# A hybrid attention and convolution layer on one core: f32 weights split at each use, a scaling moved to ScalarE, a sum moved to the DMA, loads and products moved ahead

## The chip, the cores and the metric

The kernel runs on one core of one Trainium2 chip. The metric is the device time of one execution in microseconds (us). A core has TensorE (PE in the profile; PEld is its weight load), VectorE (DVE), ScalarE (ACT), GpSimd (POOL) and SyncE (SP), which work side by side, each through its own instructions in order. DMAs are issued from the queues of SP, ACT and POOL and move data between the chip's memory (HBM) and the on-chip buffer (SBUF); matmuls write to PSUM, which has 8 banks here.

## The reference

One inference step of one layer, for 2048 prompt tokens and 32 sample tokens of 1024 values:

```
h   = rmsnorm(x);  z = h @ w_in        # q | k | v | gate_a | B | C | u | gate_c | merge_a | merge_c
q, k = rope(rmsnorm(q)), rope(rmsnorm(k))
attn = softmax with sinks, 8 q heads and 2 kv heads of 64, each chunk of 64 tokens over itself and 2 chunks before
conv = causal convolution of C * u over 3 tokens
y_a = (attn * silu(gate_a)) @ w_attn_out
y_c = (B * conv * silu(gate_c)) @ w_conv_out
r   = x + (sigmoid(merge_a) * y_a + sigmoid(merge_c) * y_c) @ w_o
out = r + sigmoid(r @ w_ple_gate) * (p @ w_ple_proj)
```

The outputs are `out`, and the newest keys, values and convolution rows.

## The kernel before

All values are f32, and everything is kept transposed: 128 features by tokens. For precision each operand of a matmul is split in two halves of the type float32r, a rounded high part and the rest (`split`, L92 to L94: ScalarE casts the high part, VectorE subtracts to get the low one; `split_half`, L96 to L98, does the same with a factor of 0.5). Each product takes three matmuls: high by high, high by low, low by high.

**The start** (L559 to L605). Rows of p are multiplied by W_pp (`p_product`, L535: 6 matmuls into a bank, ScalarE copies the bank out, a DMA on ACT's queue stores it to `z_pp`). In the program, four of the eight products of tokens 0 to 511 come before the RMS norm of the first x and four after the first step of h @ W_in.

**Phase I** (to about 885 us) computes z = h @ W_in in two halves of tokens, with 7 products in place of 8 for each 2 x 2 of blocks (`run`, L479, L364 for the matmuls). The steps (`steps`, L108 to L120) go over 21 groups of weight columns in each half. Results go to scratch tensors in HBM: `z_q`, `z_ga`, `z_y` (the convolution branch, already gated), `z_t` (tanh of the merge gates).

**Phase II** (from about 885 us) first multiplies the convolution rows by W_B for blocks 0 and 1 (`yB`, L935 to L945), then p @ W_pp for blocks 2 and 3 (L946 to L955), then yB for blocks 2 and 3. The convolution rows are loaded and split by `conv_rows` (L926): for blocks 0 and 1 at L933, at the head of Phase II; for 2 and 3 after their p products (L954). Then it goes over the four blocks of 512 tokens (the last has 32 more). In each block: finish the block's attention; yA = attention @ W_A (L968 to L978), times the gate `ta` (loaded from `z_t`), plus the convolution's share by an accumulating DMA on POOL's queue (L974); split into m; r = x + m @ W_o (L982 to L992), stored to `z_r` and split; tanh(r @ W_pg / 2) (L995 to L1011). The last step reads `pp` (p @ W_pp) and `rs` (r) back from HBM, and VectorE makes (tanh + 1) * pp (L1005) and 0.5 * that + rs (L1007); a DMA stores the row.

**Attention** is a set of generators, one for each 128 tokens (`attention`, L715, `sink_attention`, L651). It is advanced between the products by `tick` (L875), from a list of due times written by hand (`plan`, L895 to L903). A tile is transposed by PE, normed, rotated on POOL (L742 to L774), transposed again; then per chunk of 64: the scores S (L659), the maximum (L663), the exponential with its row sums on ScalarE (L675), the reciprocal of the sums (L679), P scaled by it on VectorE (L684), the transposes of P (L693), P times V (L709), the gate (L811).

**Weights.** The order of all weights is a list (`worder`, L123 to L131). A weight of 128 x 512 f32 (256 KB) is loaded on SP's queue into a buffer `wr` (`load_w`, L163), two ahead, and split into a buffer `w` (512 KB, a ring of 7, `WB`), up to 7 ahead of its use (`prefetch`, L191). The weights of Phase II (keys "q") are used up to four times: W_A, W_o and W_pg once for each block, W_B once for each pair of blocks. At its first use such a weight is split, and the split pair is stored to HBM by a DMA on POOL's queue:

```
k = wkept[key[2:]] = dram.tile([P, 2, 4, P], F32R, tag=f"wk{i}", name=f"wk{i}")
nc.gpsimd.dma_start(out=k, in_=w)                 # L207
```

At each later use the pair is loaded back on POOL's queue (L202) and nothing is split.

**Buffers and order.** Rows of a block live in a ring of 13 buffers (`tmp`), longer-lived ones in a pool of 36 (`row`, `pair`). An instruction that needs a buffer waits until the last reader of the buffer's former content is done, and all that stands behind it on its queue waits too. The order of each engine's instructions is not quite that of the program: it is fixed when the kernel is built, by a list scheduler with a model of times (L1088).

Of the kernel before, what the change touches and what calls it, by code (L numbers as in the profile page):

```python
# [8 lines left out]
F32R = mybir.dt.float32r  # L9
AF = mybir.ActivationFunctionType  # L10
# [3 lines left out]
P = 128  # L14
# [24 lines left out]
def tile_hybrid_stream_step(ctx: ExitStack, tc: tile.TileContext, x, xT, pT, wu, consts, rope, ckT, cv_dup,  # L39
# [52 lines left out]
    def split(hi, lo, src):  # L92
        nc.scalar.copy(out=hi, in_=src)  # L93
        nc.vector.tensor_tensor(out=lo, in0=src, in1=hi.bitcast(F32), op=sub)  # L94
# [36 lines left out]
        worder += [("q", b, UPG + n, s) for n in range(8) for s in range(2)]  # L131
    wsum = {g: dram.tile([P, 4, 4, P], F32, tag=f"ws{g}", name=f"ws{g}") for g in range(G)}
    WS = {7: 0, 5: 1, 6: 2, 3: 3}

    wkept = {}
    raw_of, made, used = {}, [], [0]
    raws = [0]
    ahead = [4]
# [24 lines left out]
    def load_w(i):  # L163
        key = worder[i]
        if key[0] == "q":
            return load_quad(key[2], key[3], f"wr{i}")
        if key[0] == "pp":
            return load_quad(UPP + key[2] // 2, key[2] % 2, f"wr{i}")
        _, h, g, p = key
        _, _, u1, u2 = groups[g]  # L170
        if p in (1, 2):
            return load_quad(u1, p - 1, f"wr{i}")
        if h == 0:
            if g not in sums:
# [8 lines left out]
    firsts = {}  # L183
    for i, key in enumerate(worder):
        if key[0] == "q":
            firsts.setdefault(key[2:], i)

    def kept(i):
        return worder[i][0] == "q" and firsts[worder[i][2:]] < i

    def prefetch(upto):  # L191
        upto = min(upto, len(worder))
        while len(made) < upto:
            i = len(made)
            while raws[0] < min(i + 2, len(worder)):
                if not kept(raws[0]):
                    raw_of[raws[0]] = load_w(raws[0])
                raws[0] += 1
            w = wp.tile([P, 2, 4, P], F32R, tag="w", name=f"w{i}")
            key = worder[i]  # L200
            if kept(i):
                nc.gpsimd.dma_start(out=w, in_=wkept[key[2:]])  # L202
            else:
                split(w[:, 0], w[:, 1], raw_of.pop(i))
                if key[0] == "q":
# [329 lines left out]
    def p_product(name, n, t0, q, pa, wpp):  # L535
        t = tmp(f"pp{name}_{n}")
        for c0, cn in [(0, q)] if q <= 512 else [(0, q // 2), (q // 2, q // 2)]:
            ps = bank(f"pp{name}_{n}_{c0}")
            for k in range(2):
                for e, (a, c) in enumerate(((0, 0), (0, 1), (1, 0))):  # L540
                    nc.tensor.matmul(out=ps[:, :cn], lhsT=wpp(n, a, k), rhs=pa[k][c][:, c0:c0 + cn],  # L541
                                     start=k == 0 and e == 0, stop=k == 1 and e == 2)
# [10 lines left out]
    def finish(r):  # L553
        try:
            next(r)
        except StopIteration as e:
            return e.value

    X1 = second_half()  # L559
    pa = p_rows("0", 0, 512)  # L560
# [47 lines left out]
    for i, todo in enumerate(steps):  # L608
        if i < 8:
            continue  # L610
        if todo[0][:2] == (0, 0) and todo[0][2] in (7, 5, 3, 4):
            make_x(todo[0][2])
        run(todo)
        if i in prep:
            next(X1, None)
        for p in range(1, 8):
            if last[p] == i:
                if p == 1:
                    for _ in X1:
                        pass  # L620
                refill(p)
# [20 lines left out]
    def blk(b):  # L642
        t0, npr, ns = BLOCKS[b]
        nt = npr + ns
        subs = [(0, nt)] if nt <= 512 else [(0, nt // 2), (nt // 2, nt // 2)]
        tiles = [(ns + i * P, P) for i in range(npr // P)] + ([(0, ns)] if ns else [])
        return t0, npr, ns, nt, subs, tiles

    def sink_attention(name, ng, lhs, krhs, cn, e_out, norm, keys, sk, nsk, done):  # L651
# [28 lines left out]
        for kv in range(2):  # L680
            for j in range(ng):
                g = kv * ng + j
                for src, dst in norm(kv, j):
                    nc.vector.tensor_scalar(out=dst, in0=src, scalar1=se[:, g:g + 1], scalar2=None, op0=mul)  # L684
        yield
        w = ng * P
        pts = []
# [226 lines left out]
                nc.tensor.matmul(out=ps[:, :cn], lhsT=lo, rhs=a[0][:, c0:c0 + cn], start=False, stop=(i == n - 1))  # L914
        return [(ps, c0, cn) for ps, (c0, cn) in zip(pss, subs)]

    def load_row(name, src, b):
        t0, nt = BLOCKS[b][0], blk(b)[3]
        t = tmp(name)
        nc.sync.dma_start(out=t[:, :nt], in_=src[:, t0:t0 + nt])  # L920
        return t


    yc = {}

    def conv_rows(b):  # L926
        nt = blk(b)[3]
        for c in range(4):
            t = load_row(f"yc{b}_{c}", z_y[c], b)
            yc[b, c] = pair(f"ycs{b}_{c}")  # L930
            split_half(yc[b, c][0][:, :nt], yc[b, c][1][:, :nt], t[:, :nt])
# [25 lines left out]
    for b in range(len(BLOCKS)):  # L957
        t0, npr, ns, nt, subs, tiles = blk(b)
        last = b == len(BLOCKS) - 1
        finish_attention(b)  # L960
        ac = []
        for j in range(4):
            a = pair(f"ac{b}_{j}")
            split_half(a[0][:, :nt], a[1][:, :nt], ats[b][j][:, :nt])
            ac.append(a)

        mT = []
        for n in range(8):  # L968
            ta = load_row(f"ta{b}_{n}", z_t[0][n], b)
            w = next_w(("q", b, UY + n, 0))  # L970
            for ps, c0, cn in product(f"yA{b}_{n}", [w], ac, subs):
                nc.vector.scalar_tensor_tensor(out=ta[:, c0:c0 + cn], in0=ta[:, c0:c0 + cn], scalar=1.0,  # L972
                                               in1=ps[:, :cn], op0=add, op1=mul)
            nc.gpsimd.dma_start(out=ta[:, :nt], in_=z_t[1][n][:, t0:t0 + nt], accum_op=add)  # L974
            m = pair(f"m{b}_{n}")
            split_half(m[0][:, :nt], m[1][:, :nt], ta[:, :nt])
            mT.append(m)
            tick(2.8)  # L978


        rT = []
        for n in range(8):  # L982
            xr = tmp(f"xr{b}_{n}")
            nc.sync.dma_start(out=xr[:, :nt], in_=xT[n * P:(n + 1) * P, t0:t0 + nt])
            w = [next_w(("q", b, UO + n, s)) for s in range(2)]
            for ps, c0, cn in product(f"o{b}_{n}", w, mT, subs):
                nc.vector.tensor_tensor(out=xr[:, c0:c0 + cn], in0=ps[:, :cn], in1=xr[:, c0:c0 + cn], op=add)
            r = pair(f"r{b}_{n}")
            split(r[0][:, :nt], r[1][:, :nt], xr[:, :nt])
            nc.gpsimd.dma_start(out=z_r[n][:, t0:t0 + nt], in_=xr[:, :nt])  # L990
            rT.append(r)
            tick(5.6)  # L992


        for n in range(8):  # L995
            tg = tmp(f"tg{b}_{n}")
            pp = load_row(f"zp{b}_{n}", z_pp[n], b)
            rs = load_row(f"rsum{b}_{n}", z_r[n], b)
            w = [next_w(("q", b, UPG + n, i)) for i in range(2)]
            cut = last and n == 7  # L1000
            for ps, c0, cn in product(f"pg{b}_{n}", w, rT, subs):
                nc.scalar.activation(out=tg[:, c0:c0 + cn], in_=ps[:, :cn], func=AF.Tanh, scale=0.5)
                for o0, on in ([(c0, cn)] if cut else [(0, nt)] if c0 + cn == nt else []):
                    o = slice(o0, o0 + on)
                    nc.vector.scalar_tensor_tensor(out=tg[:, o], in0=tg[:, o], scalar=1.0, in1=pp[:, o],  # L1005
                                                   op0=add, op1=mul)
                    nc.vector.scalar_tensor_tensor(out=rs[:, o], in0=tg[:, o], scalar=0.5, in1=rs[:, o],  # L1007
                                                   op0=mul, op1=add)
# [89 lines left out]
```

## Time and profile before

| what | us |
|---|---|
| median of 3 runs | 1615.51 |
| lowest, highest | 1613.94, 1619.77 |
| the profiled execution | 1621.73 |
| its span, first to last instruction | 1620.0 |
| PE, DVE, ACT and POOL busy in it | 1563.2, 981.6, 628.8, 446.9 |

The profile shows one execution. Its page gives the busy time of each engine; further views give the same for chosen stretches with the clock that TensorE was granted and the load of the DMA engines, the groups of instructions (line, engine, operation, output <- inputs, shapes, count, busy us, mean ns, then the idle time before them and what ended it), who waited for whom, and the chain of work that ended last. Matmuls overlap, so that the mean of one is longer than the distance between two. L numbers are lines of the kernel before.

### The profile page before, as it was taken

What the parts mean: (1) busy time and instruction counts of PE and PEld (TensorE: products, weight loads), DVE (VectorE), ACT (ScalarE), POOL (GpSimd) and SP (SyncE); (2) the same over time, 40 slices, a digit from 0 to 9 for tenths busy, and PEclk for the clock granted to TensorE, in tenths of its full rate; (3) what the DMA queues carried; (4) which work ended last, traced back from release to release, by engine and by line L of the source; (5) the groups of instructions that cost most, each with busy time, mean ns of one, the idle gap of its engine ahead of it and who ended that gap; (6) DMA issues with size and microseconds to landing.
All of it is one profiled execution on the core that took longest, in us unless ns stands there. A gap on an engine that the chain in (4) does not pass through costs nothing.

```text
span 1620.0 us, 26331 instructions
## 1 busy us (share of the span) xinstructions
PE 1563.2 (96%) x9387; PEld 1391.0 (86%) x9387; DVE 981.6 (61%) x1932; ACT 628.8 (39%) x1470; POOL 446.9 (28%) x676
## 2 busy tenths in 40 slices
PE   6899999999999999999999999988998999999998
PEld 5688888888899999999999788966886888788998
DVE  7875667756763455554333676777877777764322
ACT  6544334543563333333444364344433334432111
POOL 3122112212100000010000561544455455642320
PEclk8999999999999999999999999998999999999999
DMA  7655446689885433334446977898988789979986
GB/s 260 227 197 187 153 153 198 221 276 317 299 271 162 131 110 105 105 112 139 145 144 201 357 233 237 313 265 279 315 284 209 252 291 300 252 235 330 287 283 208
DMA packets 176691, 366.21 MB, mean 226 GB/s; under 512 B 21296, under 2 KB 44400, under 8 KB 176560
## 3 DMA queue, kind: packets, MB, share of 16 engines
q1 hardware_dynamic: 111312, 169.78, 33.2%
q0 software_dynamic: 50560, 167.59, 31.9%
q10 hardware_dynamic: 14688, 27.16, 4.4%
q8 instruction: 74, 1.21, 0.3%
q14 instruction: 57, 0.47, 0.1%
HBM read 243.50 MB, written 121.05 MB: 225 GB/s over the span
## 4 chain that ended last, share of the span: by engine, by line
PE 76%; issue 12%; DMA 6%; DVE 4%; ACT 1%; SPq 1%; POOL 0%; ACTq 0%; DVEq 0%; POOLq 0%
PE a L370 8%; PE a L372 8%; PE a L375 8%; PE c L370 4%; PE c L372 4%; PE c L375 4%; PE ps_pg L911 3%; PE ps_pg L912 3%; PE ps_pg L914 3%; PE ps_o L912 3%; PE ps_o L911 3%; PE ps_o L914 3%; PE pp L541 2%; DMA ta<-z_t 2%; PE b L370 2%
## 5 line engine op out<-in xcount | busy, mean ns | idle before, releaser
L370 PE MATMUL a<-x_h,w 128*128 128x264 f32 (+1 forms) x1008 | 309.6, 322 | 3.0 <-ACT x_h L93 2.6
L372 PE MATMUL a<-x_l,w 128*128 128x264 f32 (+1 forms) x1008 | 310.1, 321 | 0.0
L375 PE MATMUL a<-x_h,w 128*128 128x264 f32 (+1 forms) x1008 | 268.6, 320 | 0.0
L94 DVE TENSOR_TENSOR w<-wr,w 128x512 fp32r<-128x512 f32 x241 | 178.4, 741 | 144.5 <-ACT w L93 121.5
L93 ACT CAST w<-wr 128x512 fp32r<-128x512 f32 x241 | 149.9, 624 | 219.3 <-PE c L375 82.3
L370 PEld LDWEIGHTS a<-x_h,w 128*128 128x128 f32 x1008 | 190.0, 189 | 18.2 <-ACT x_h L93 3.0
L372 PEld LDWEIGHTS a<-x_l,w 128*128 128x128 f32 x1008 | 189.8, 188 | 14.3
L375 PEld LDWEIGHTS a<-x_h,w 128*128 128x128 f32 x1008 | 167.5, 188 | 14.7
L370 PE MATMUL c<-x_h,w 128*128 128x264 f32 (+1 forms) x504 | 155.1, 321 | 0.0
L372 PE MATMUL c<-x_l,w 128*128 128x264 f32 (+1 forms) x504 | 154.6, 320 | 0.0
L375 PE MATMUL c<-x_h,w 128*128 128x264 f32 (+1 forms) x504 | 133.7, 320 | 0.0
L202 POOL DMA_DIRECT2D w<-wk x128 | 75.3, 589 | 149.1 <-PE ps_o L914 60.8
L504 DVE SCALAR_TENSOR_TENSOR u<-u,c 128x264 f32<-128x264 f32 (+1 forms) x126 | 61.1, 512 | 88.0 <-ACT u L499 52.2
L911 PE MATMUL ps_o<-m_h,w 128*128 128x512 f32 (+1 forms) x320 | 109.9, 363 | 4.0 <-DVE ta L972 2.3
L911 PE MATMUL ps_pg<-r_h,w 128*128 128x512 f32 (+1 forms) x320 | 111.5, 356 | 0.4 <-ACT r_h L93 0.4
L912 PE MATMUL ps_o<-m_l,w 128*128 128x512 f32 (+1 forms) x320 | 110.6, 358 | 0.6 <-DVE m_l L98 0.5
L912 PE MATMUL ps_pg<-r_l,w 128*128 128x512 f32 (+1 forms) x320 | 110.2, 352 | 0.0
L914 PE MATMUL ps_o<-m_h,w 128*128 128x512 f32 (+1 forms) x320 | 103.9, 357 | 0.0
L914 PE MATMUL ps_pg<-r_h,w 128*128 128x512 f32 (+1 forms) x320 | 102.0, 351 | 0.0
L372 PEld LDWEIGHTS c<-x_l,w 128*128 128x128 f32 x504 | 95.0, 188 | 7.1
L370 PEld LDWEIGHTS c<-x_h,w 128*128 128x128 f32 x504 | 94.8, 188 | 7.2
L499 ACT COPY u<-a 128x264 f32<-128x264 f32 (+1 forms) x126 | 51.9, 450 | 104.4 <-PE a L375 103.5
(246 smaller groups left out, 3488.1 us busy)
## 6 DMA issues: line engine op xcount, KB each, us to landing
w<-wk POOLq DMA_DIRECT2D x128, 512.0 KB, 5.4
wr<-in_wu SPq DMA_DIRECT2D x157, 256.0 KB, 3.5
wk<-w POOLq DMA_DIRECT2D x48, 512.0 KB, 6.6
a<-in_wu SPq DMA_DIRECT2D x84, 256.0 KB, 3.1
wr<-ws SPq DMA_DIRECT2D x84, 256.0 KB, 2.9
ws<-a POOLq DMA_DIRECT2D x63, 256.0 KB, 3.7
xr<-xc SPq DMA_DIRECT2D x28, 264.0 KB, 5.5
z_pp<-pp ACTq DMA_DIRECT2D x24, 256.0 KB, 3.2
```

Source lines behind the costliest of these rows:

```text
L93: nc.scalar.copy(out=hi, in_=src)
L94: nc.vector.tensor_tensor(out=lo, in0=src, in1=hi.bitcast(F32), op=sub)
L202: nc.gpsimd.dma_start(out=w, in_=wkept[key[2:]])
L370: nc.tensor.matmul(out=ps[:, :cn], lhsT=w[:, 0, k], rhs=x[0][:, c0:c0 + cn], start=first and k == 0, stop=False, skip_group_check=True)
L372: nc.tensor.matmul(out=ps[:, :cn], lhsT=w[:, 0, k], rhs=x[1][:, c0:c0 + cn], start=False, stop=False, skip_group_check=True)
L375: nc.tensor.matmul(out=ps[:, :cn], lhsT=w[:, 1, k], rhs=x[0][:, c0:c0 + cn], start=False, stop=k == 3, skip_group_check=True)
L499: nc.scalar.copy(out=t[:, c0:c0 + cn], in_=ps[:, :cn])
L504: nc.vector.scalar_tensor_tensor(out=t[:, c0:c0 + cn], in0=t[:, c0:c0 + cn], scalar=-1.0, in1=ps[:, :cn], op0=mul, op1=sub)
L541: nc.tensor.matmul(out=ps[:, :cn], lhsT=wpp(n, a, k), rhs=pa[k][c][:, c0:c0 + cn], start=k == 0 and e == 0, stop=k == 1 and e == 2)
L911: nc.tensor.matmul(out=ps[:, :cn], lhsT=hi, rhs=a[0][:, c0:c0 + cn], start=(i == 0), stop=False)
L912: nc.tensor.matmul(out=ps[:, :cn], lhsT=hi, rhs=a[1][:, c0:c0 + cn], start=False, stop=False)
L914: nc.tensor.matmul(out=ps[:, :cn], lhsT=lo, rhs=a[0][:, c0:c0 + cn], start=False, stop=(i == n - 1))
```

## The change

Five edits:

1. The split weights are no longer kept in HBM: neither stored at the first use nor loaded back. Each use loads the f32 weight on SP's queue and splits it on ScalarE and VectorE, so 128 more loads and splits, and 128 reloads and 48 stores fewer.
2. P is scaled by ScalarE (an activation with a scale for each partition) where VectorE did it.
3. In blocks 0 to 2, r is no longer loaded by SP and added by VectorE: an accumulating DMA on POOL's queue adds `z_r` onto the row, and the DMA that stores the row comes after it on the same queue. In block 3, r is loaded as before and added by VectorE. The factor 0.5 moves into `p_product`, whose copy becomes a multiplication.
4. The convolution rows of blocks 0 and 1 are loaded and split in Phase I, right after the step with product 2 of its last group, nine steps before its end.
5. At the start, six in place of four of the products p @ W_pp of tokens 0 to 511 come before the norm of x, and two after the first step.

```diff
-    wkept = {}
...
             while raws[0] < min(i + 2, len(worder)):
-                if not kept(raws[0]):
-                    raw_of[raws[0]] = load_w(raws[0])
+                raw_of[raws[0]] = load_w(raws[0])
                 raws[0] += 1
             w = wp.tile([P, 2, 4, P], F32R, tag="w", name=f"w{i}")
-            key = worder[i]
-            if kept(i):
-                nc.gpsimd.dma_start(out=w, in_=wkept[key[2:]])
-            else:
-                split(w[:, 0], w[:, 1], raw_of.pop(i))
-                if key[0] == "q":
-                    k = wkept[key[2:]] = dram.tile([P, 2, 4, P], F32R, tag=f"wk{i}", name=f"wk{i}")
-                    nc.gpsimd.dma_start(out=k, in_=w)
+            split(w[:, 0], w[:, 1], raw_of.pop(i))
             made.append(w)
...
-            nc.scalar.copy(out=t[:, c0:c0 + cn], in_=ps[:, :cn])
+            nc.scalar.mul(out=t[:, c0:c0 + cn], in_=ps[:, :cn], mul=0.5)
...
-    for n in range(4):
+    for n in range(6):
         p_product("0", n, 0, 512, pa, wpp_of)
...
-    for n in range(4, 8):
+    for n in range(6, 8):
         p_product("0", n, 0, 512, pa, wpp_of)
...
         run(todo)
+        if todo[0] == (1, G - 1, 2):
+            conv_rows(0)
+            conv_rows(1)
...
-                    nc.vector.tensor_scalar(out=dst, in0=src, scalar1=se[:, g:g + 1], scalar2=None, op0=mul)
+                    nc.scalar.activation(out=dst, in_=src, func=AF.Copy, scale=se[:, g:g + 1])
...
-    conv_rows(0)
-    conv_rows(1)
...
-            rs = load_row(f"rsum{b}_{n}", z_r[n], b)
+            rs = load_row(f"rsum{b}_{n}", z_r[n], b) if last else None
...
-                    nc.vector.scalar_tensor_tensor(out=rs[:, o], in0=tg[:, o], scalar=0.5, in1=rs[:, o],
-                                                   op0=mul, op1=add)
+                    if last:
+                        nc.vector.tensor_tensor(out=tg[:, o], in0=tg[:, o], in1=rs[:, o], op=add)
+                    else:
+                        nc.gpsimd.dma_start(out=tg[:, o], in_=z_r[n][:, t0 + o0:t0 + o0 + on], accum_op=add)
                     (nc.sync if last else nc.gpsimd).dma_start(
-                        out=yT[n * P:(n + 1) * P, t0 + o0:t0 + o0 + on], in_=rs[:, o])
+                        out=yT[n * P:(n + 1) * P, t0 + o0:t0 + o0 + on], in_=tg[:, o])
```

More of the change, by code (lines that the diff above doesn't have):

```diff
@@ L181, in load_w @@
         return t
-    firsts = {}
-    for i, key in enumerate(worder):
-        if key[0] == "q":
-            firsts.setdefault(key[2:], i)
-    def kept(i):
-        return worder[i][0] == "q" and firsts[worder[i][2:]] < i
     def prefetch(upto):
@@ L195, in prefetch @@
             while raws[0] < min(i + 2, len(worder)):
-                if not kept(raws[0]):
-                    raw_of[raws[0]] = load_w(raws[0])
+                raw_of[raws[0]] = load_w(raws[0])
                 raws[0] += 1
             w = wp.tile([P, 2, 4, P], F32R, tag="w", name=f"w{i}")
-            key = worder[i]
-            if kept(i):
-                nc.gpsimd.dma_start(out=w, in_=wkept[key[2:]])
-            else:
-                split(w[:, 0], w[:, 1], raw_of.pop(i))
-                if key[0] == "q":
-                    k = wkept[key[2:]] = dram.tile([P, 2, 4, P], F32R, tag=f"wk{i}", name=f"wk{i}")
-                    nc.gpsimd.dma_start(out=k, in_=w)
+            split(w[:, 0], w[:, 1], raw_of.pop(i))
             made.append(w)
@@ L557, in finish, with blk, load_row, conv_rows @@
             return e.value
+    def blk(b):
+        t0, npr, ns = BLOCKS[b]
+        nt = npr + ns
+        subs = [(0, nt)] if nt <= 512 else [(0, nt // 2), (nt // 2, nt // 2)]
+        tiles = [(ns + i * P, P) for i in range(npr // P)] + ([(0, ns)] if ns else [])
+        return t0, npr, ns, nt, subs, tiles
+    def load_row(name, src, b):
+        t0, nt = BLOCKS[b][0], blk(b)[3]
+        t = tmp(name)
+        nc.sync.dma_start(out=t[:, :nt], in_=src[:, t0:t0 + nt])
+        return t
+    yc = {}
+    def conv_rows(b):
+        nt = blk(b)[3]
+        for c in range(4):
+            t = load_row(f"yc{b}_{c}", z_y[c], b)
+            yc[b, c] = pair(f"ycs{b}_{c}")
+            split_half(yc[b, c][0][:, :nt], yc[b, c][1][:, :nt], t[:, :nt])
     X1 = second_half()
@@ L639, in tile_hybrid_stream_step @@
         nc.gpsimd.memset(v.bitcast(F32), 0.0)
[L642 to L647, printed above, removed]
     def sink_attention(name, ng, lhs, krhs, cn, e_out, norm, keys, sk, nsk, done):
@@ L915, in product @@
         return [(ps, c0, cn) for ps, (c0, cn) in zip(pss, subs)]
[L917 to L931, printed above, removed]
-    conv_rows(0)
-    conv_rows(1)
     for b0 in (0, 2):
```

## The prediction

> **What bounds the kernel now.** I read the page first, then busy time, clock and DMA of the second half stage by stage, then TensorE's waits there, then the chain of waits around each of its stops.
>
> ```profile
> PE 1563.2 (96%) x9387; PEld 1391.0 (86%) x9387; DVE 981.6 (61%) x1932; ACT 628.8 (39%) x1470; POOL 446.9 (28%) x676
> ```
>
> TensorE is busy for 96% of the span, so no change that leaves the matmuls alone can win more than its idle time and the time at a lower clock. The stage table says where these lie (columns: stretch, its length, busy time of PE, PEld, DVE, ACT and POOL, then the clock, the DMA share and GB/s). The stretches are a sample of the first half; its end with the first yB part; p @ W_pp; the second yB part; blocks 0, 1, 2 and 3; and the whole second half.
>
> ```profile
> 240.00:280.00 40.00, 40.00 (x175) 32.56 (x174) 28.21 (x48) 19.28 (x43) 8.08 (x14) 1.00 0.63 207
> 885.00:895.00 10.00, 6.43 (x51) 6.00 (x49) 3.62 (x7) 4.14 (x9) 4.10 (x7) 1.00 0.98 299
> 895.00:947.00 52.00, 51.50 (x239) 41.84 (x240) 38.31 (x69) 18.64 (x48) 32.41 (x38) 0.97 0.98 338
> 947.00:981.50 34.50, 33.30 (x231) 30.66 (x230) 27.27 (x82) 25.37 (x84) 15.41 (x22) 1.00 0.74 233
> 981.50:1046.50 65.00, 62.21 (x402) 57.58 (x400) 41.23 (x111) 22.90 (x69) 20.44 (x30) 0.95 0.80 273
> 1046.50:1201.50 155.00, 142.18 (x706) 118.47 (x705) 116.86 (x253) 65.87 (x177) 72.78 (x99) 0.94 0.88 282
> 1201.50:1352.60 151.10, 143.59 (x728) 119.50 (x727) 110.31 (x233) 51.73 (x159) 79.62 (x105) 0.98 0.86 267
> 1352.60:1494.60 142.00, 138.96 (x713) 115.64 (x713) 90.48 (x233) 49.64 (x155) 66.82 (x95) 1.00 0.89 271
> 1494.60:1615.20 120.60, 120.45 (x961) 120.23 (x959) 34.92 (x64) 16.04 (x32) 30.17 (x51) 1.00 0.87 268
> 885.00:1615.20 730.20, 698.62 (x4016) 609.92 (x4014) 462.99 (x1048) 254.33 (x730) 321.75 (x444) 0.98 0.87 276
> ```
>
> In the sample PE is full with the DMA at 0.63. In the second half PE idles 730.20 - 698.62 = 31.6 us with the DMA at 0.87. A clock below 1.00 costs length times what is missing: 52.0 x 0.03, 65.0 x 0.05, 155.0 x 0.06 and 151.1 x 0.02, together 1.6 + 3.3 + 9.3 + 3.0 = 17.2 us. So at most 48.8 us are to be had here; the stretches with a low clock are those with the long stops. The Trainium skill (TensorE: Matmul & The Clock Gate, Part 1) says that an idle window of about 3.4 us halves the clock and a busy one of the same length restores it. By that alone, five stops would cost half of 3.4 us each, 8.5 us in all, and my forecast would gain some 7 us less; the rows say 17.2, and I go by them.
>
> Which wait ends last at the stops (waits of PE, second half; then pieces of the chain: start, us, what):
>
> ```profile
> PE pq L730 <- DMA zq<-z_q: 7.3, 2, 6.1
> PE ps_yB L911 <- ACT ycs_h L97: 6.4, 3, 3.5
> PE S L659 <- DVE ta L972: 5.2, 2, 3.8
> ...
> PE pk L783 <- POOL kr L770: 0.5, 1, 0.5
> ```
>
> ```profile
> 889.63 9.47 DMA yc<-z_y
> 980.77 6.56 DMA yc<-z_y
> 1066.96 12.85 DMA ta<-z_t
> 1112.91 13.22 DMA zkv<-z_q
> 1230.03 13.77 DMA ta<-z_t
> ```
>
> ScalarE and VectorE are named in the first list, but the chain shows a load behind each large stop, issued 6 to 14 us before it landed. The second half waits for a full DMA.
>
> **The change: traffic.** The weight rows (name, issues, KB each, us to landing):
>
> ```profile
> w<-wk POOLq DMA_DIRECT2D x128, 512.0 KB, 5.4
> wk<-w POOLq DMA_DIRECT2D x48, 512.0 KB, 6.6
> wr<-ws SPq DMA_DIRECT2D x84, 256.0 KB, 2.9
> ta<-z_t POOLq DMA_DIRECT2D x24, 256.0 KB, 6.5
> ```
>
> The 128 reloads of split weights (67.1 MB) and the 48 stores (25.2 MB) go; 128 f32 loads (33.6 MB) come: 58.7 MB less of 276 GB/s x 730.2 us = 201.5 MB. Over some 700 us that leaves 204 GB/s, the rate of the first half's row, where PE never stopped; loads of the first half land in 2.9 us (wr<-ws). I therefore expect most late landings to go, in the stretches where they cost.
>
> **Terms of gain.** Leaving Phase I (885 to 947): 3.6 + 0.5 idle and 1.6 of clock = 5.7 us; the conv rows of blocks 0 and 1 are now loaded and split some nine steps earlier, while PE is full, and the stop at 889 to 899 has nothing left to wait for: 5. What hides their eight splits is that first half (DVE 28.21 of 40); without it they would cost what they do now. Second yB part: 2.8 + 3.3 = 6.1; its load (980.77) is not moved and was issued late as well as landing late, so I take half, 3. Block 0: 12.8 + 9.3 = 22.1; its stops follow the landings at 1066.96 and 1112.91, and I take 17. Block 1: 7.5 + 3.0 = 10.5, most of it behind 1230.03: 8. Block 2: 3.0, with no landing of that kind in its chain: 1. Block 3: PE is full, nothing.
>
> The start:
>
> ```profile
> 20.42 1.11 PE L252 MATMUL rps<-cst,dg 128*128 128x128 f32 x4 [3.16 <-DVE dg L250]
> 24.14 1.65 PE L370 MATMUL a<-x_h,w 128*128 128x512 f32 x3 [2.61 <-ACT x_h L93]
> 25.79 6.76 PE pp L541 x24
> 29.03 8.60 DVE L94 TENSOR_TENSOR x_l<-b,x_h 128x512 fp32r<-128x512 f32 x5
> ```
>
> Two of the four products between 25.79 and 32.55 move into the idle 3.16 + 2.61 us. That frees 6.76 / 2 = 3.4 us, but the steps behind need x_l, which only begins at 29.03; I take 2, bounds 0 and 3.4. Sum of gains: 2 + 5 + 3 + 17 + 8 + 1 = 36.
>
> **Terms of cost.** Rows of single instructions in the second half (line, engine, operation, shapes, count, then busy us, mean ns, idle before):
>
> ```profile
> L684 DVE TENSOR_SCALAR P<-P,se 128x192 f32<-128x192 f32 x120 | 52.5, 495 | 0.6
> L94 DVE TENSOR_TENSOR w<-wr,w 128x512 fp32r<-128x512 f32 x50 | 45.7, 915 | 10.1 <-ACT w L93 10.0
> L1007 DVE SCALAR_TENSOR_TENSOR rsum<-tg,rsum 128x512 f32<-128x512 f32 x24 | 19.7, 823 | 0.4
> L675 ACT ACTIVATE P<-S,nmm 128x192 f32<-128x192 f32 x120 | 49.0, 421 | 41.7 <-DVE nmm L666 39.6 <-PE O L710 1.8
> L93 ACT CAST w<-wr 128x512 fp32r<-128x512 f32 x50 | 30.9, 619 | 62.4 <-PE ps_yB L914 26.7 <-PE ps_o L914 14.3 <-issue 6.5
> L675 ACT ACTIVATION_READ_ACCUMULATOR P<-S,nmm 128x1 f32 x128 | 26.1, 204 | 0.0
> L202 POOL DMA_DIRECT2D w<-wk x128 | 75.3, 589 | 149.1 <-PE ps_o L914 60.8 <-PE ps_pg L914 53.6 <-PE ps_yA L914 7.1
> ```
>
> The same split in the first half, its cast over the whole run, and the part of block 2 in which VectorE is fullest:
>
> ```profile
> L94 DVE TENSOR_TENSOR w<-wr,w 128x512 fp32r<-128x512 f32 x152 | 104.8, 690 | 95.5 <-ACT w L93 72.7 <-DMA wr<-ws 17.3 <-DMA wr<-in_wu 3.9
> L93 ACT CAST w<-wr 128x512 fp32r<-128x512 f32 x241 | 149.9, 624 | 219.3 <-PE c L375 82.3
> 1383.00:1443.00 60.00, 58.34 (x313) 48.90 (x311) 45.38 (x119) 22.98 (x73) 35.02 (x49) 1.00 0.85 249
> ```
>
> VectorE: + 128 x 0.69 to 0.915 = 88 to 117 us; minus the P scaling, 52.5, and 24 additions, 19.7; net + 16 to 45 over 730, on 463. ScalarE: + 128 x 0.62 = 79 and 120 scalings. No row shows such a scaling on ScalarE; the nearest is the exponential of the same shape, 0.42, and the bounds are 0.20 (reading its accumulator) and 0.62 (a 512-wide cast): + 24 to 74, I take 50. That makes about 383 of 700. Neither engine is full on average. Block 0 already splits every weight and scales P on VectorE, which stands at 116.86 of 155.0 there, and its largest stops are behind loads. Tightest is the W_o part of block 2: 45.38 + 16 x 0.69 less some 20 scalings at 0.3 gives 50 of 60. New waits come too. A cast waits on ScalarE for a weight buffer that PE must free: 62.4 us over 50, so 160 us over 128 more, with exponentials, tanh and the casts of m and r queued behind. The first half has the same wait (219.3 - 62.4 = 157 us over 191 casts) with PE full, because the casts run up to 7 buffers ahead. The scaling waits there for VectorE's reciprocal, with the same work behind it; what it gives back is VectorE's time ahead of the transposes. I charge 3 us for all of this, bounds - 3 and 10.
>
> In the stage of p @ W_pp (947 to 981) ScalarE has 25.37 of 34.50; 16 scalings at 0.42 and about 5 casts at 0.62 bring it to 35. It evicts every product there. I charge 2, bounds 0 and 5. The multiplication by 0.5 in that eviction replaces a copy of the same shape: nothing.
>
> r by DMA: 24 loads on SP's queue become 24 accumulating transfers on POOL's, whose like lands in 6.5 us, and the store of y, next on that queue, waits for it: POOL can be held 24 x 6.5 = 156 us, with the attention's powers and rotations behind it. But the reloads that leave held POOL for 149.1 us already, waiting for weight buffers, and PE waited 0.5 us for POOL. An exchange of like for like: I charge 1, bounds - 3 (SP and the row buffers are relieved) and 10. SP's queue issues 104 loads more in sum. At the end of Phase I eight row loads now stand in it ahead of the last weights: a weight lasts 12 matmuls of 40.00 / 175 = 0.229 us, 2.7 us, and up to 7 are ahead, so even a landing of 13.77 us is covered: nothing. Costs: 3 + 2 + 1 = 6. Net - 30.
>
> The sum is made against the profiled execution: span 1620.0, with what lies around it 1621.73, 6.2 above the median 1615.51. 30 us of 1621.73 are 1.85%; on the median that gives **1586**.
>
> **Rivals.**
> - *Late landings stay.* If bursts of loads and the waits for buffers make them, not the weights' bytes, then only the start and the conv rows gain: 2 + 5, less 3 for ScalarE: 1611. For it: the 980 stop waits for a buffer too. Against: each late load shares a DMA at 0.8 to 1.0 of full.
> - *Casts and splits take over.* The splits averaged 915 ns in the second half against 690 in the first. If all 128 go at 915, that is 29 us more of DVE; if half reaches PE, and the p stage costs 5, the net is - 36 + 15 + 5 + 1 = - 15: 1601. The Trainium skill (SBUF — State Buffer, the rules on ports) gives the reason: a VectorE instruction with two SBUF inputs and a GpSimd one that reads SBUF lock each other out for the whole instruction, and the splits are of that kind; by the same rule the scaling of P, in a two-port mode, leaves the contest. Against: ScalarE and VectorE together keep slack in every stage but one.
> - *Slower: POOL held by its own accumulation.* In the W_pg parts of blocks 0 to 2 it is blocked 8 x 6.5 = 52 us each, nearly the whole part. If a third of the 156 us reaches PE through keys that are rotated late, the net is - 36 + 5 + 52 = + 21: 1636. It decides from a fifth (31 us) on. Against it stands the like-for-like hold above.
>
> **How the numbers follow.** Forecast 0.62, late landings 0.13, casts and splits 0.17, POOL 0.08. A difference under 0.5% (8 us) can't be told from none with this kernel. Faster takes the forecast, most of the third case and a third of the second, 0.80; the same 0.12; slower 0.08. All 48.8 + 3.4 of the gains without cost would give 1563, which I don't expect whole; the range is 1568 to 1610, and the cases beyond 1610 hold some 0.15.
>
> **What would show it.** Right: DMA near 200 GB/s after 885; landings of ta, zq and zkv mostly under 7 us; PE idle there under 12 us and the clock at 0.99 or more; no stop before the first yB. Wrong: PE waiting for kr or ss (POOL), or for pp's eviction; DVE over 0.95 in block 2. If the rate falls to 200 and PE still idles 25 us, the traffic was not the cause.

## The result and the profile after

The changed kernel takes 1637.22 us (median of 4 runs, 1633.46 to 1639.52), the kernel before 1617.64 beside it: ratio 1.0121, 95% interval 1.0088 to 1.0154. The forecast was 1586; the kernel became slower, by 19.6 us.

The stages of the changed kernel, in the columns of the prediction's stage table: the end of the first half with the first yB part; p @ W_pp with the second yB part; blocks 0, 1, 2, 3; and the whole second half.

```profile
PE 1570.0 (96%) x9387; PEld 1391.4 (85%) x9387; DVE 1010.9 (62%) x1904; ACT 741.0 (45%) x1730; POOL 375.1 (23%) x524
```

```profile
885.00:938.00 53.00, 53.00 (x281) 44.94 (x280) 33.94 (x61) 17.13 (x49) 36.08 (x42) 1.00 0.85 280
938.00:1040.00 102.00, 94.11 (x623) 86.07 (x622) 64.95 (x171) 61.07 (x188) 27.48 (x37) 0.98 0.62 211
1040.00:1191.30 151.30, 142.34 (x705) 116.92 (x702) 109.58 (x216) 77.81 (x211) 56.14 (x64) 0.98 0.62 171
1191.30:1354.30 163.00, 146.44 (x728) 121.14 (x729) 116.23 (x232) 83.48 (x231) 65.36 (x71) 0.97 0.64 175
1354.30:1511.10 156.80, 146.07 (x717) 120.08 (x716) 105.72 (x236) 84.99 (x236) 54.46 (x65) 0.96 0.65 176
1511.10:1632.60 121.50, 120.73 (x960) 120.08 (x959) 56.13 (x97) 35.88 (x66) 13.30 (x19) 1.00 0.62 191
885.00:1632.60 747.60, 702.70 (x4003) 609.24 (x4001) 486.55 (x1009) 360.36 (x978) 252.82 (x296) 0.98 0.65 189
```

Set against the rows of before, the first yB part ends 9.0 us earlier (938.0 for 947.0). The next stage takes 102.0 for 99.5, block 0 151.3 for 155.0, block 1 163.0 for 151.1, block 2 156.8 for 142.0, block 3 121.5 for 120.6: with the 9.0, + 17.4 in sum. The traffic fell as forecast, from 276 to 189 GB/s. But PE's idle time in the second half rose from 31.6 to 747.60 - 702.70 = 44.9 us, and the low clock costs 102.0 x 0.02 + 151.3 x 0.02 + 163.0 x 0.03 + 156.8 x 0.04 = 16.2 us, for 17.2. The prediction's own sentence for this was that then "the traffic was not the cause".

The landings of the changed kernel (output <- input, queue, issues, KB, median us from issue to landing) are short, as wanted:

```profile
wr<-in_wu SPq DMA_DIRECT2D x285, 256.0 KB, 3.4
...
ta<-z_t SPq DMA_DIRECT2D x24, 256.0 KB, 5.4
ta<-z_t POOLq DMA_DIRECT2D x24, 256.0 KB, 5.1
...
zq<-z_q SPq DMA_DIRECT2D x16, 256.0 KB, 4.9
```

What PE waits for in the changed kernel from 885 on (us in total, times, longest):

```profile
PE ps_o L911 <- ACT m_h L97: 10.3, 6, 2.8
PE ps_o L911 <- DVE ta L955: 5.9, 2, 3.1
PE ps_yB L911 <- ACT ycs_h L97: 3.8, 1, 3.8
PE ps_yA L912 <- DVE ac_l L98: 2.9, 1, 2.9
PE pq L730 <- DMA zq<-z_q: 2.9, 1, 2.9
```

The wait for zq, largest before (7.3 us), has shrunk to 2.9; the waits for m, at the step from W_A to W_o, have grown to 16.2 us. The two rows of before for that step make 3.8:

```profile
PE ps_o L911 <- DVE ta L972: 2.3, 1, 2.3
...
PE ps_o L911 <- ACT m_h L97: 1.5, 2, 1.1
```

The queues of SP and POOL, first before (SP only), then after:

```profile
SPq L145 <- DVE w L94: 67.2, 17, 11.2
```

```profile
SPq L143 <- DVE w L94: 310.6, 107, 13.3
...
POOL out_yT L994 <- DMA tg<-z_r: 74.5, 20, 5.3
```

SP's queue stood still for 310.6 us until the split of an older weight freed a buffer, and what is issued behind a waiting load waits too. POOL stood for 74.5 us until an accumulated row had landed. A piece of the chain of waits at the end of block 1 shows that hold on the path (start, us, what):

```profile
1340.94 5.82 DMA tg<-z_r
...
1347.05 0.56 POOL out_yT L994
1347.62 2.02 POOL ss L742
...
1349.66 0.04 DVE qn L747
```

POOL's power for the next norm starts only after the row's sum has landed and its store has been issued. Both queues are candidates; whether either is the cause is for the experiments.

### The profile page after: what moved, and what is told of

Its sections match the earlier page's. It is cut to its first block, busy times and chain, and to the rows that moved or that the text cites. A ratio compares the mean times of both kernels' runs of the same rounds, so it can differ in the third digit from the quotient of the medians.

```text
span 1637.5 us, 26529 instructions
## 1 busy us (share of the span) xinstructions
PE 1570.0 (96%) x9387; PEld 1391.4 (85%) x9387; DVE 1010.9 (62%) x1904; ACT 741.0 (45%) x1730; POOL 375.1 (23%) x524
## 5 line engine op out<-in xcount | busy, mean ns | idle before, releaser
L94 DVE TENSOR_TENSOR w<-wr,w 128x512 fp32r<-128x512 f32 x369 | 284.0, 771 | 178.0 <-ACT w L93 154.0
L93 ACT CAST w<-wr 128x512 fp32r<-128x512 f32 x369 | 228.5, 622 | 251.7 <-PE c L357 80.6
L352 PE MATMUL c<-x_h,w 128*128 128x264 f32 (+1 forms) x504 | 155.1, 321 | 0.0
L911 PE MATMUL ps_o<-m_h,w 128*128 128x512 f32 (+1 forms) x320 | 113.2, 366 | 16.2 <-ACT m_h L97 10.3
L914 PE MATMUL ps_o<-m_h,w 128*128 128x512 f32 (+1 forms) x320 | 104.1, 359 | 0.0
L352 PEld LDWEIGHTS c<-x_h,w 128*128 128x128 f32 x504 | 94.8, 188 | 7.2
L357 PEld LDWEIGHTS c<-x_h,w 128*128 128x128 f32 x504 | 83.5, 188 | 7.5
```

What stands on the lines that cost most here:

```text
L352: nc.tensor.matmul(out=ps[:, :cn], lhsT=w[:, 0, k], rhs=x[0][:, c0:c0 + cn], start=first and k == 0, stop=False, skip_group_check=True)
L357: nc.tensor.matmul(out=ps[:, :cn], lhsT=w[:, 1, k], rhs=x[0][:, c0:c0 + cn], start=False, stop=k == 3, skip_group_check=True)
L911: nc.tensor.matmul(out=ps[:, :cn], lhsT=hi, rhs=a[0][:, c0:c0 + cn], start=(i == 0), stop=False)
```

## The experiments

Two theories stand from here on for edit 1: the loads on SP's in-order queue (*queue*) and the work of casting and subtracting on ScalarE and VectorE (*work*). For edit 3: the wait for the landing (*hold*), or the accumulating transfer itself (*accumulation*). Ratios are to the kernel before, on the same chip. The two kernels that set the questions undo edits 3 and 1.

**r by VectorE again** (edits 1, 2, 4, 5):

```diff
-            rs = load_row(f"rsum{b}_{n}", z_r[n], b) if last else None
+            rs = load_row(f"rsum{b}_{n}", z_r[n], b)
...
-                        nc.gpsimd.dma_start(out=tg[:, o], in_=z_r[n][:, t0 + o0:t0 + o0 + on], accum_op=add)
+                    nc.vector.tensor_tensor(out=tg[:, o], in0=tg[:, o], in1=rs[:, o], op=add)
```

> The changed kernel with edit 3 undone: r is loaded by SP and added by VectorE in all four blocks; the other four edits stay. Theory P (POOL is held while the store of y waits for the accumulation, 70.8 us of waits in the profile after, and the attention's powers and ta's accumulations stand behind it): the loss goes, about 1600 us or less. Theory S (SP's queue stands still while weight loads wait for buffers that VectorE's splits must free, some 230 us of waits, and the loads of ta, zp and zq stand behind them): the loss stays, 1630 to 1645 us, since 24 more loads come onto the same queue.

Measured 1.0006 (0.9990 to 1.0022). Edit 3 costs 1.0121 - 1.0006 = 1.15%, 18.6 us of 1620.

**Split pairs kept** (edits 2, 3, 4, 5; L191 to L209 as before), **and edit 1 alone** (the kernel before with the changed `prefetch`):

> The changed kernel with edit 1 undone: the split weights are stored and loaded back on POOL's queue as before; the other four edits stay. Theory S: SP runs ahead again, the loss goes, 1595 to 1610 us (start, conv rows and the scaling on ScalarE gain). Theory P: the accumulation now shares POOL with the reloads, so the loss stays or grows, 1635 us or more.

> The kernel before with edit 1 alone: f32 weights loaded and split at each use, nothing else. Theory S: slower than before, 1630 to 1650 us, as VectorE also still scales P and adds r. Theory P: no accumulation of r, so the saved traffic shows: 1590 to 1605 us.

Measured 1.0053 (1.0035 to 1.0070) and 1.0055 (1.0035 to 1.0076), which is 1629 us each, and 1621 for the kernel before these two. None of the three lies in a range that was expected of it: edits 1 and 3 both cost. The f32 weights, the largest gain in my sum, are a loss by themselves.

**Kept pairs and r by VectorE** (edits 2, 4, 5), then **edits 4 and 5 alone** (P scaled by VectorE again) and **edit 2 alone**:

> The changed kernel with edits 1 and 3 undone: only the scaling on ScalarE, the conv rows ahead and the products first remain. Both theories: faster than before by the start and the conv rows, about 5 to 10 us, 1605 to 1612 us. If it is over 1616, one of these three edits costs by itself.

> The kernel before with the conv rows loaded ahead and more of p @ W_pp first, nothing else. If the gains of x4 (0.9912) are those of the moves alone and P on ScalarE adds what it did alone (0.9984): 0.993. The prediction's terms for these two moves were 2 + 5 us, 0.9957. If the scaling of P on ScalarE is needed for the blocks: 0.996 to 0.998.

> The kernel before with edit 2 alone: P scaled by ScalarE. If it carries block 1's recovery in the run with edits 2, 4 and 5 (149 to 140 us there): 0.993 to 0.996. If the recovery was the conv rows' or the start's doing: 0.998 to 1.002.

Measured 0.9912 (0.9884 to 0.9939), 0.9965 (0.9947 to 0.9983) and 0.9984 (0.9963 to 1.0005; not clear of no change). So there is a chain in which one edit is added at a time, with 1% as 16.2 us:

| step | ratio | us |
|---|---|---|
| edits 4 and 5 | 0.9965 | -5.7 |
| + edit 2, P on ScalarE | 0.9912 | -8.6 |
| + edit 1, f32 weights | 1.0006 | +15.2 |
| + edit 3, r by DMA | 1.0121 | +18.6 |

Each step carries some 3 to 6 us of uncertainty from the intervals, and its size may depend on the order: edit 2 alone gave 2.6 us.

**The parts of edit 1.** Four kernels lie between the kept pairs (0.9912) and the f32 weights (1.0006). All four leave out the low halves of repeated weights: the third matmul reads the high half again, so that TensorE's work stays, and the output is not the reference's. The first keeps and reloads only the high halves:

```diff
-                nc.gpsimd.dma_start(out=w, in_=wkept[key[2:]])
+                nc.gpsimd.dma_start(out=w[:, 0], in_=wkept[key[2:]])
```

> The kernel with edits 2, 4 and 5 (0.9912), which keeps split weights, but only the high half is stored and loaded back (256 KB in place of 512 KB each way, 46 MB less); the third matmul of a repeated weight reads the high part in place of the low one, so PE's work stays and the output is not the reference's. ScalarE, VectorE and the number of transfers are as they were. Only the traffic falls. If the DMA's load was what made the late landings, as the prediction has it: 0.978 to 0.985. If not: 0.989 to 0.993.

The second issues these reloads on SP's queue (`nc.sync` in place of `nc.gpsimd`):

> As the kernel that keeps and reloads only the high halves (its third matmul reads the high half too, so the low halves of repeated weights play no part), but the reloads stand on SP's queue in place of POOL's; the bytes are the same, and no cast or split is added. Theory A, the loads of weights on SP's in-order queue wait for buffers and the rows of the block (ta, pp, zq) wait behind them: it gives back most of what that kernel had won over the kernel with the cast kept, 0.992 to 0.997. Theory B, ScalarE's casts of the repeated weights are what cost: it stays at 0.986, within 0.003.

The third loads the f32 weights there and casts them, without the subtraction:

```diff
-            split(w[:, 0], w[:, 1], raw_of.pop(i))
...
+            if key[0] == "q" and key[2:] in seen:
+                nc.scalar.copy(out=w[:, 0], in_=raw_of.pop(i))
...
+            else:
+                split(w[:, 0], w[:, 1], raw_of.pop(i))
...
```

> The kernel of the run with r on VectorE (edits 1, 2, 4, 5), but at each repeated use of a weight VectorE's half of the split is left out: 128 subtractions fewer; the third matmul reads the high part in place of the low one, so that PE's work stays and the output is not the reference's. Loads and ScalarE's casts stay. Theory D: the loss of edit 1 goes, and the lower traffic may show: ratio 0.980 to 0.992. Theory S: the loads then wait for ScalarE's casts in place of the subtractions, half of the loss at most goes: 0.995 to 1.000. If ScalarE's 128 casts are the cost: 0.999 to 1.003.

The fourth moves that cast to VectorE:

> As the f32 kernel without low halves of repeated weights (r by load and VectorE, the third matmul reads the high half), but the cast of a repeated weight is done by VectorE, not ScalarE. Loads and queues stay the same. Theory A (SP's queue): 0.995 as that kernel, within 0.003. Theory B (ScalarE's casts hold the exponentials, the scaling and the evictions behind them): 0.986 to 0.990, with ScalarE's share in the blocks falling from 0.68 to about 0.55.

Measured: 0.9862 (0.9811 to 0.9913), 0.9942 (0.9927 to 0.9958), 0.9953 (0.9939 to 0.9968), 0.9958 (0.9945 to 0.9972). The first lies between the two ranges that were expected of it. The steps, in us, each with the uncertainty that the two intervals leave: half the bytes - 8.1 (9 either way, so perhaps nothing); from POOL's queue to SP's + 13.0 (9 either way); f32 and casts + 1.8 (3.5 either way, so not clear of none); VectorE's subtractions (the f32 kernel with them is the 1.0006 above) + 8.6 (3.5 either way); in sum + 15.3. No cost of the cast shows, on either engine. The *queue* is the largest step, and of the *work* it is the subtraction that shows a cost. The stage rows (885 to the end), first of the kernel with half the bytes on POOL's queue, then of the one with the whole pairs:

```profile
885.00:1591.00 706.00, 688.54 (x4005) 602.85 (x4003) 420.32 (x905) 290.25 (x850) 317.55 (x443) 0.99 0.74 217
```

```profile
885.00:1602.00 717.00, 692.00 (x4004) 607.69 (x4003) 406.38 (x906) 291.51 (x849) 320.86 (x444) 0.98 0.87 277
```

Idle 17.5 us for 25.0: traffic at 217 GB/s in place of 277 is worth 8 us, give or take 9, not the 29 that my sum drew from it. And SP's waits when the same reloads stand there, which the kernel with the reloads on POOL doesn't have:

```profile
SPq L202 <- PE ps_o L934: 129.4, 44, 14.0
SPq L202 <- PE ps_pg L934: 104.1, 46, 16.3
```

Two limits of these steps. Here SP waits for matmuls to free a weight buffer; in the f32 kernels it waits for a cast or a split to free a raw one, so the 13.0 us are shown for these reloads alone. And the sum of such waits is no price: SP waits for splits and casts 329.2 us without the repeated subtractions (237.1 + 92.1) and 306.9 with them, where the time is 8.6 us longer:

```profile
SPq L144 <- ACT w L192: 237.1, 85, 9.9
SPq L144 <- DVE w L94: 92.1, 28, 12.6
```

```profile
SPq L143 <- DVE w L94: 306.9, 108, 13.2
```

So SP's waits do not account for the subtractions' 8.6 us. The 175 of the second half took 0.85 us each on average in that kernel; the first half's row of before has 0.69. Whether their own time or the work that waits behind them is the price is open.

**What in SP's queue comes late?** Three attempts to take the cost away. The raw buffers in the order in which they became free; the f32 loads on POOL's queue; the block's rows ta and x loaded two and one products earlier, with f32 weights, and the same with kept pairs as a control:

```diff
-            return load_quad(key[2], key[3], f"wr{i}")
+            t = quad(f"wr{i}")
+            nc.gpsimd.dma_start(out=t, in_=wu[key[2], :, 4 * key[3]:4 * key[3] + 4, :])
+            return t
...
-            ta = load_row(f"ta{b}_{n}", z_t[0][n], b)
+            need_ta(n + 2)
...
+            ta = tas[n]
```

> The kernel of the run with r on VectorE (edits 1, 2, 4, 5), and the nine buffers for f32 weights are reused in order of the longest free, so that no load on SP's queue has to wait for a split just ahead of it. Theory S (SP's queue stands still behind those waits, and the row loads with it): ratio to before 0.990 to 0.995, about 1605 to 1612 us. Theory D (VectorE itself: 128 more subtractions in its queue, ahead of the work that the changes of stage wait for): no change, ratio 0.998 to 1.003.

> The kernel of the run with r on VectorE (edits 1, 2, 4, 5; 1.0006), with the f32 weights of Phase II loaded by POOL's queue in place of SP's, so that the loads of rows no longer stand behind weights that wait for buffers. Theory S (SP's queue): 0.990 to 0.995. Theory D (VectorE's 128 subtractions in its queue): 0.998 to 1.003. If POOL held by those waits costs what SP held did, 1.000 or more as well, and then the profile must show POOL's waits in front of PE's.

> The changed kernel with r added by VectorE (its time was 1.0006), in which the loads of ta stand two products earlier on SP's queue in each block, and those of x for r one product earlier. Theory A, that the f32 weight loads wait for buffers on this queue and the block's rows wait behind them: the stops of PE on m and ta go, 0.992 to 0.997. If the rows are not what comes late through this queue: 1.000 within 0.002.

> The same earlier loads of ta and x in the kernel that keeps the split pairs (its time was 0.9912, and SP hardly waits for weights there). Theory A: no change from 0.9912, within 0.002, or a little better if the loads of ta that landed late under the full DMA gain by it: 0.988. If earlier rows help here as much as in the f32 kernel: 0.985 or less, and the queue is not what sets the two apart.

Measured 1.0019 (1.0005 to 1.0034), 0.9997 (0.9978 to 1.0017), 1.0010 (0.9996 to 1.0024) and 0.9956 (0.9940 to 0.9972), the first three against 1.0006, the last against 0.9912. None wins, and with kept pairs the earlier rows lose 7 us, give or take 5, which was not expected. The theory of SP's queue had asked for 0.990 to 0.995 in the first two and 0.992 to 0.997 in the third, and missed all three. With the f32 loads on POOL, block 0 falls from 151.4 to 141.1 us, and block 2 rises from 154.8 to 168.1; POOL now does the waiting:

```profile
POOL wr L165 <- DVE w L94: 175.6, 71, 8.1
```

With the rows ahead, block 0 falls by 5.9 and block 2 rises by 2.8, and the median stays. So it is shown that the place of the reloads costs 13 us (9 either way), and not shown by which item behind them; loading the rows of ta and x earlier does not take the cost away, and moving the f32 loads to POOL does not either. The order of all instructions is fixed when the kernel is built and changes with every edit, so these kernels differ in more than the edited line. The traces show it: the kernels with whole and with half the bytes have the same instructions, but their order on VectorE and ScalarE differs in places. How much of a step of some us is that order is open.

**Edit 3: hold or accumulation?** The store of y on SP's queue in blocks 0 to 2, so that POOL need not wait for the landing:

```diff
-                    (nc.sync if last else nc.gpsimd).dma_start(
+                    nc.sync.dma_start(
```

> The changed kernel; only the queue of y's stores in blocks 0 to 2 differs: SP in place of POOL, so that POOL issues the accumulation and goes on, and SP waits for its landing. Theory P (POOL held): the loss of edit 3 goes, ratio from 1.012 to 0.999 to 1.004. Rival: the accumulation is slow whoever waits (longer use of the row buffers, contention), or SP held is as bad as POOL held: 1.010 or more.

Measured 1.0123 (1.0092 to 1.0153): no change. The hold moves to the queue with the weights (the whole second half):

```profile
SPq L143 <- DVE w L94: 242.5, 89, 13.4
SPq L994 <- DMA tg<-z_r: 82.7, 24, 6.3
```

Then r is stored into the output, and the row is accumulated onto it in HBM, so that nothing waits for that landing; first with kept pairs, then with f32 weights:

```diff
-                        nc.gpsimd.dma_start(out=tg[:, o], in_=z_r[n][:, t0 + o0:t0 + o0 + on], accum_op=add)
-                    (nc.sync if last else nc.gpsimd).dma_start(
-                        out=yT[n * P:(n + 1) * P, t0 + o0:t0 + o0 + on], in_=tg[:, o])
+                        nc.gpsimd.dma_start(out=yT[n * P:(n + 1) * P, t0 + o0:t0 + o0 + on], in_=tg[:, o],
+                                            accum_op=add)
...
```

> The changed kernel with edit 1 undone, and edit 3 in another form: in blocks 0 to 2 r is stored into the output itself, and the gated row is accumulated onto it there, so that no instruction waits for the accumulation and there is one transfer in place of two. Theory P: the loss of edit 3 (1.0053 against 0.9912 without it) goes: 0.988 to 0.992. Rival (accumulating costs as such): 1.000 or more.

> The changed kernel with the sum of r in the form in which nothing waits: r is stored into the output and the row added onto it by one accumulating transfer in HBM. If the two costs (f32 weights; the held POOL queue) add up: 0.9963 + 0.0094 = 1.0057. If POOL's queue, freed of the reloads, takes the accumulations without a loss: 1.000 or less. With the accumulation at fault in either form: 1.012.

Measured 0.9963 (0.9950 to 0.9976) and 1.0091 (1.0066 to 1.0115). With kept pairs the cost of edit 3 is 1.0053 - 0.9912, 22.8 us, and this form takes back 14.6 of it. With f32 weights it takes back 4.9 of 18.6, and the intervals overlap. Both lie between the ranges that were expected. In the f32 kernels the loss sits in block 1: 163.1 us with edit 3, 161.8 in this form, 165.7 with the store on SP, 149.2 with VectorE's sum. So with kept pairs the wait is part of the cost, or the second transfer is, since this form has neither; with f32 weights that is not shown. In both, the accumulation in HBM costs 8 to 14 us with nothing behind it waiting. Why is open. One thing speaks against reading POOL's waits as a price: in the kernel at 1.0006 the same store waits as long, for VectorE's sum.

```profile
POOL out_yT L991 <- DVE tg L990: 86.4, 16, 8.7
```

**A version from the parts**: kept pairs and r by VectorE, with W_B always loaded as f32 and W_o stored only at its second use:

```diff
-        if key[0] == "q":
+        if key[0] == "q" and not (key[2] < UO and key[3] == 1) and not (UO <= key[2] < UPG and key[1] == 0):
             firsts.setdefault(key[2:], i)
...
```

> The kernel with edits 2, 4 and 5, in which f32 weights are split again only where it relieves the first uses: W_B is loaded as f32 both times and never stored, and W_o is split in blocks 0 and 1 and stored in block 1 only. All other weights are kept as before. If the stores crowd the DMA in block 0 (14 us idle and 8 us of clock there): 0.984 to 0.989. If the 24 more splits cost what they save: 0.990 to 0.994.

Measured 0.9894 (0.9850 to 0.9938), the same as 0.9912 within the intervals. Both beat the kernel before and the changed one.

## Why the prediction was wrong

Stage lengths in us from the traces (ends of the yB parts and of the W_pg products). Each trace is one execution; that of edits 2, 4, 5 is 3.6 us longer than the median of its kernel, that of half the bytes on POOL 2.0 shorter.

| kernel | to first yB | p, second yB | block 0 | 1 | 2 | 3 |
|---|---|---|---|---|---|---|
| before | 947.1 | 99.0 | 155.1 | 151.2 | 142.3 | 120.3 |
| edits 4, 5 | 936.4 | 103.0 | 155.4 | 148.1 | 142.2 | 120.2 |
| edit 2 alone | 949.8 | 103.8 | 157.6 | 139.2 | 141.1 | 120.3 |
| edits 2, 4, 5 | 938.4 | 105.4 | 156.6 | 140.5 | 141.2 | 120.2 |
| half the bytes, POOL | 938.2 | 97.9 | 149.8 | 138.6 | 146.3 | 120.3 |
| half the bytes, SP | 938.1 | 97.5 | 150.9 | 148.0 | 147.9 | 122.1 |
| f32, cast only | 939.3 | 100.8 | 150.7 | 147.3 | 148.8 | 121.3 |
| edits 1, 2, 4, 5 | 936.7 | 101.9 | 151.4 | 149.2 | 154.8 | 124.2 |
| all (after) | 937.7 | 102.3 | 151.3 | 163.1 | 156.7 | 121.5 |

- **Start, 2 us, and conv rows, 5 us: right.** The first yB part ends 9.0 us earlier in the changed trace, and these two edits alone are worth 5.7 us in the median. PE has no stop from 885 to 938: it is busy for 53.00 of 53.00.
- **Traffic falls to 204 GB/s: right** (189). **"I therefore expect most late landings to go": right too.** The failed step is the next one, that the stops go with them: "its stops follow the landings at 1066.96 and 1112.91, and I take 17", and 8 for block 1. The chain named the late load as what ended last, and I booked the whole stop to it. With half the bytes block 0 gained 6.8 us and block 1 1.9, the stage before them gained 7.5 and block 2 lost 5.1: 8.1 in the median, in place of 29. One row I read loosely: the load at 1112.91 (zkv) landed at 1126.13, while PE's stop of 6.13 us ended at 1124.82, with zq, issued 1.4 us ahead of it; the burst is the same.
- **Block 1's stop went without less traffic.** The chain was right that its largest stop, 2.28 us, ended with a late load: ta landed at 1243.80, and PE went on at 1244.66. But the block shrank from 151.2 to 139.2 with edit 2 alone, and from 148.1 to 140.5 with edit 2 on top of edits 4 and 5, with all reloads in place; in the trace of edit 2 alone PE stops nowhere in it for more than 0.4 us. The other stages took most of that back there: 2.7, 4.8 and 2.5 us up to the end of block 0, where I had charged 2 for the p stage. How edit 2 takes the stop away is open. A candidate is what VectorE's scalings meet: in the trace of before, the first of four scalings of P took 6.22 us in block 1, where the median is 0.34, as POOL ran its rotations (first the line over the block, with shortest, median and longest in ns; then start, us, engine, line):

```profile
L684 DVE TENSOR_SCALAR P<-P,se x32: 328/338/6224, 1211.2 to 1328.6; 128x192 f32<-128x192 f32 x32
```

```profile
1251.04 6.99 DVE L684 TENSOR_SCALAR P<-P,se 128x192 f32<-128x192 f32 x4
```

```profile
1251.09 3.11 POOL L766 TENSOR_TENSOR tt<-qn,ab 128x1024 f32<-128x1024 f32 x2
1254.13 1.44 POOL L774 TENSOR_TENSOR qr<-tt 128x256 f32<-128x256 f32 x2
1255.52 0.89 POOL L770 TENSOR_TENSOR kr<-tt 128x128 f32<-128x128 f32 x2
1256.37 0.74 POOL L744 TENSOR_TENSOR ab<-cs,cst 128x256 f32<-128x256 f32 x1
```

  PE did not stop behind this row, so it is not shown to be what edit 2 gained. I had costed what edit 2 adds to ScalarE (50 us of busy time; it took 44.9) and given its removal from VectorE no gain of its own. The Trainium skill (SBUF — State Buffer, Who interferes with whom) says that a VectorE instruction in a two-port mode and a GpSimd one exclude each other for the whole instruction. I used it for a rival only; the row agrees with it, and no run here separates it from another cause.
- **"I charge 3 us for all of this"** (casts, splits, new waits): the term was sized by engine shares, "Neither engine is full on average". VectorE's subtractions cost 8.6 us, though in the changed kernel VectorE is busy for only 109.58 of 151.3 us in block 0 and 116.23 of 163.0 in block 1. The casts, whose waits I had counted at 160 us, show no cost.
- **SP's queue, charged at nothing:** the step failed. I counted its 104 more loads and looked only at the end of Phase I. What I left out is that a load waits, on an in-order queue, for a buffer that is freed late: 310.6 us of waits in place of 67.2. The price of such a place is shown for the half reloads, 13.0 us between the two queues; for the f32 loads it is argued from that.
- **"An exchange of like for like: I charge 1"** for r by DMA: it cost 18.6. The reloads had held POOL as long, without harm: the kernel that keeps them gains. Equal sums of waiting were no measure; what makes the difference is open.
- **The sum.** I had - 7 for edits 4 and 5, + 2 for edit 2, - 26 for edit 1 (29 of traffic less 3) and + 1 for edit 3, net - 30. The chain gives - 5.7, - 8.6, + 15.2 and + 18.6: + 19.5. The rival "POOL held by its own accumulation" named 1636 and 8% and comes nearest to 1637 by luck: its mechanism is at most a part of the 18.6, and it gave edit 1 the full gain, where edit 1 cost 15.2.

## What to carry to other kernels

A late load that ends a stop is not the whole price of the stop: take the load away in thought and ask what is late next, and price the bytes by a run that halves them and changes as little else as can be. A DMA put on an in-order queue can cost more than its issue time (13 us here for the same 128 reloads on another queue); so write down, for each load, which event frees its buffer and what stands behind it. A short VectorE instruction beside GpSimd ones took up to 6.22 us in place of 0.34 here, so a move off VectorE is worth pricing even where VectorE is not full. And a step of a few us between two kernels needs its interval beside it: halving the bytes gave 8 us with 9 either way.

## What the runs showed of the hardware

One subtraction with 4 values in each partition took 3.19 us on VectorE in the changed kernel, as POOL ran its rotations (mean of the 32 of its shape: 0.40 us, median 0.16):

```profile
1392.11 3.19 DVE L666 SCALAR_TENSOR_TENSOR nmm<-nm,nsink_sb 128x4 f32<-128x4 f32 x1
```

```profile
1392.10 1.68 POOL L774 TENSOR_TENSOR qr<-tt 128x256 f32<-128x256 f32 x2
1393.48 1.11 POOL L770 TENSOR_TENSOR kr<-tt 128x128 f32<-128x128 f32 x2
1394.30 0.97 POOL L744 TENSOR_TENSOR ab<-cs,cst 128x256 f32<-128x256 f32 x1
```

It began with the first of these POOL instructions and ended as the last of them was done, as did the scaling of 6.22 us above, which ran from 1251.04 to 1257.26 beside POOL's from 1251.09 to 1257.11. The same scaling of P that VectorE had done in 478 to 495 ns on average, with such outliers, took ScalarE 449 ns on average over all 120 cases, and between 438 and 467 ns in the 96 of them from block 0 on in the kernel with edit 2 alone.

The accumulating transfers of r (256 KB) landed in 5.3 us (median) at 189 GB/s in the changed kernel and in 6.0 at 269 in that with split pairs kept, those of ta in 5.1 and 6.9: with the DMA share 0.2 lower, such a transfer landed an eighth to a quarter sooner.
